# Sharing the products of the first three slots between VectorE and ScalarE, and issuing the fourth load behind the third group

## The chip, the core and the metric

The kernel runs on one core of a Trainium2 chip. Four of its engines matter here. VectorE (DVE in the profile) and ScalarE (ACT) compute; SyncE (SP) computes nothing and issues transfers; ScalarE issues transfers too, from the same instruction stream as its arithmetic. The transfers themselves run on the core's 16 DMA engines. They are fed by two queues: q1 holds what SyncE issued, q10 what ScalarE issued. An engine runs its instructions in order; an instruction that waits holds up all that stand behind it on that engine.

The metric is the time of the kernel on the device in microseconds (us), the median of several runs. The profile shows one further execution, whose own time stands beside its span below.

## The reference

For each of 16 x 1024 tokens there is a row of 512 fp32 numbers and two fp32 weights. The result has, for each token, two rows of 512: the token's row times its first weight and times its second. `expert_indices` is not used.

```python
batch, seq, hidden, n_experts = 16, 1024, 512, 8
k = 2
x_expanded = x[:, :, np.newaxis, :].repeat(k, axis=2)
weights = expert_weights[..., np.newaxis]
return (x_expanded * weights).astype(np.float32)
```

33.55 MB are read and 67.11 MB are written, and each element read is multiplied twice.

## The kernel before

The 16384 tokens are cut into 8 groups of 2048. In a group each of the 128 partitions holds 16 consecutive tokens (T = 16). There are three slots in SBUF, and group i uses slot i mod 3. A slot has 64 KB in each partition, which is 16384 fp32 numbers: room for the 16 x 2 product rows of a group. The load of a group (4 MB) brings the 16 x-rows of each partition into the upper half of the slot, numbers 8192 to 16383. The products are then written in place over the whole slot: token t reads 512 numbers from 8192 + 512 t and writes 1024 numbers from 1024 t. So the products of tokens 0 to 7 go into the free lower half, and those of the tokens behind them overwrite x-rows that must have been used: token 11 writes over the rows of tokens 6 and 7, token 12 over those of 8 and 9, token 13 over 10 and 11, token 14 over 12 and 13, and token 15 over 14 and its own.

`products` (line 133) is one VectorE instruction, a `tensor_tensor` multiply for a run of tokens lo to hi, with the weights broadcast along the row. `ranges` (line 123) cuts the 16 tokens into runs of 8, 4, 2 and 1, so that no run overwrites a row that it still reads; with the 16th token left, `last` (line 151) does its two products on ScalarE, two instructions of 128 x 512, the second of them in place. They come after all four VectorE instructions of the group.

Stores go out on SyncE: one of 8 MB for a whole group (line 178), but for the first group and the last group two of 4 MB, of which the first (line 174) follows the run of 8 tokens. Loads go out on ScalarE (line 120). The first three loads are issued at the start. Load i + 2 stands in ScalarE's stream behind the two products of group i, for i from 1, and it waits there until the stores of group i - 1, which used the same slot, have landed. So ScalarE's stream is: loads 0, 1, 2; two products of group 0; two of group 1; load 3; two of group 2; load 4; two of group 3; load 5; and so on. The order of all instructions is that of the program, since the kernel schedules by hand (line 104).

Ahead of the groups, the weights (128 KB) are loaded on SyncE and turned into their layout `w_tile` by TensorE transposes and three VectorE copies (lines 66 to 102).

Of the kernel before, what the change touches and what calls it, by code (L numbers as in the profile page):

```python
# [1 line left out]

# [4 lines left out]


@with_exitstack
def kernel(  # L10
    ctx: ExitStack,
    tc: tile.TileContext,
    x: bass.AP,
    expert_indices: bass.AP,
    expert_weights: bass.AP,
    out: bass.AP,
):
    nc = tc.nc

    batch, seq, hidden = x.shape  # L20
    k = expert_weights.shape[-1]
    P = nc.NUM_PARTITIONS
    ntok = batch * seq
    assert ntok % P == 0

    f32 = mybir.dt.float32
    row = k * hidden


    groups = [16] * 8  # L30
    assert sum(groups) * P == ntok
    TX = max(groups)

    xf = x.rearrange("b s h -> (b s) h")
    of = out.rearrange("b s k h -> (b s) (k h)")
    wf = expert_weights.rearrange("b s k -> (b s) k")

    w_pool = ctx.enter_context(tc.tile_pool(name="w_pool", bufs=1))
    slots = ctx.enter_context(tc.tile_pool(name="slots", bufs=3))
    raw_pool = ctx.enter_context(tc.tile_pool(name="raw_pool", bufs=1))  # L40
    psum = ctx.enter_context(
        tc.tile_pool(name="psum", bufs=2, space=bass.MemoryType.PSUM)
    )

    w_tile = w_pool.tile([P, sum(groups) * k], f32)

    def rows(flat, done, T):
        return flat[done * P : (done + T) * P, :].rearrange("(p a) n -> p (a n)", a=T)

    B = 8
    M = P // B
    ident = w_pool.tile([P, P], f32)
    nc.gpsimd.memset(ident, 0.0)  # L55
    nc.gpsimd.affine_select(  # L56
        out=ident,
        in_=ident,
        compare_op=mybir.AluOpType.not_equal,
        fill=1.0,  # L60
        base=0,
        pattern=[[-1, P]],
        channel_multiplier=1,
    )

    def weights_in(head, G, T):
        raw_tile = raw_pool.tile([G * M, B * T * k], f32, name=f"raw{T}_tile")
        nc.sync.dma_start(
            out=raw_tile,
            in_=wf[head * P : (head + G * T) * P, :].rearrange(  # L70
                "(q a) n -> q (a n)", a=B * T
            ),
        )
        return raw_tile

    def weights_spread(raw_tile, head, G, T):
        n = T * k
        col_tile = raw_pool.tile([n, G * P], f32, name=f"col{T}_tile")
        cols = col_tile.rearrange("c (q r) -> c q r", r=B)
        step = 4  # L80
        for r0 in range(0, B, step):
            up_tile = psum.tile([n, step, G * M], f32)
            for r in range(step):
                nc.tensor.transpose(  # L84
                    up_tile[:, r, :],
                    raw_tile[:, (r0 + r) * n : (r0 + r + 1) * n],
                    ident[: G * M, : G * M],
                )
            nc.vector.tensor_copy(  # L89
                out=cols[:, :, r0 : r0 + step],  # L90
                in_=up_tile.rearrange("c r q -> c q r"),
            )
        down_tile = psum.tile([P, G * n], f32)
        for g in range(G):
            nc.tensor.transpose(  # L95
                down_tile[:, g * n : (g + 1) * n],
                col_tile[:, g * P : (g + 1) * P],
                ident[:n, :n],
            )
        nc.vector.tensor_copy(  # L100
            out=w_tile[:, head * k : (head + G * T) * k], in_=down_tile
        )

    ctx.enter_context(tc.manual_schedule())

    starts = [sum(groups[:i]) for i in range(len(groups))]
    loaded = []

    def load(i):
        if i >= len(groups):
            return
        T = groups[i]
        slot_tile = slots.tile([P, TX * row], f32)
        loaded.append(slot_tile)
        src = rows(xf, starts[i], T)
        at = T * (row - hidden)
        nc.scalar.dma_start(out=slot_tile[:, at : at + T * hidden], in_=src)  # L120


    def ranges(T):
        lo, out = 0, []
        while lo < T - 1:
            hi = lo + 1
            while (hi + 1) * k <= T * (k - 1) + lo and hi < T - 1:
                hi += 1
            out.append((lo, hi))
            lo = hi  # L130
        return out

    def products(slot_tile, T, lo, hi, w_at):
        m = hi - lo
        at = T * (row - hidden) + lo * hidden
        nc.vector.tensor_tensor(  # L136
            out=slot_tile[:, lo * row : hi * row].rearrange(
                "p (t k h) -> p t k h", t=m, k=k
            ),
            in0=slot_tile[:, at : at + m * hidden]  # L140
            .rearrange("p (t h) -> p t h", t=m)
            .unsqueeze(2)
            .to_broadcast([P, m, k, hidden]),
            in1=w_tile[:, w_at + lo * k : w_at + hi * k]
            .rearrange("p (t k) -> p t k", t=m)
            .unsqueeze(3)
            .to_broadcast([P, m, k, hidden]),
            op=mybir.AluOpType.mult,
        )

    def last(slot_tile, T, w_at):
        for c in range(T * k - k, T * k):
            nc.scalar.mul(  # L153
                out=slot_tile[:, c * hidden : (c + 1) * hidden],
                in_=slot_tile[:, T * row - hidden : T * row],
                mul=w_tile[:, w_at + c : w_at + c + 1],
            )

    raw_tile = weights_in(0, 8, 16)
    load(0)  # L160
    load(1)
    load(2)
    weights_spread(raw_tile, 0, 8, 16)

    for i, T in enumerate(groups):
        slot_tile = loaded[i]
        outr = rows(of, starts[i], T)
        w_at = starts[i] * k
        done = 0
        for lo, hi in ranges(T):  # L170
            products(slot_tile, T, lo, hi, w_at)
            if i in (0, len(groups) - 1) and done == 0:
                done = hi
                nc.sync.dma_start(
                    out=outr[:, : done * row], in_=slot_tile[:, : done * row]
                )
        last(slot_tile, T, w_at)
        nc.sync.dma_start(
            out=outr[:, done * row :], in_=slot_tile[:, done * row : T * row]
        )  # L180
        if i:
            load(i + 2)

# [1 line left out]
_INS = ['x', 'expert_indices', 'expert_weights']  # L185
_OUTS = [((16, 1024, 2, 512), 'float32')]


# [23 lines left out]
```

## Time and profile before

| what | value |
|---|---|
| median of three runs | 242.16 us (239.26 to 251.51; 239.26, 242.16, 251.51) |
| the profiled execution's own time | 239.3 us |
| its span in the profile | 237.5 us |
| VectorE busy | 134.7 us (57%) |
| ScalarE busy | 12.8 us (5%) |
| TensorE busy | 2.9 us |
| moved by DMA | 100.80 MB, 424 GB/s over the span |
| the 16 DMA engines' time, q1 and q10 | 65.5% and 33.2% |

Times in the rows of the profile count from the start of the span. In a row of the timeline the first number is the start, the second the length, "x4" means four instructions merged, and the bracket tells how long the engine had been idle and what ended that. An issue ("ACTq", "SPq") is the short instruction that hands a transfer to its queue; the transfer runs on by itself and "lands" when its semaphore has been raised by all 16 engines. In a table of windows the columns are: the stretch, its length, the busy time of PE, PEld, DVE, ACT and POOL with the number of instructions, the granted TensorE clock, the busy share of the 16 DMA engines and the rate in GB/s. The share can pass 1.00 a little, since a packet's bytes and time are booked at one place.

### The profile page before, as it was taken

Reading aid. Unit: us, or ns where it says so; the run is one execution under the profiler, and the core shown is the slowest. Engines: PE = TensorE matmul, PEld = TensorE weight load, DVE = VectorE, ACT = ScalarE, POOL = GpSimd, SP = SyncE. Lnnn points to the kernel's source line nnn. Section 1 sums busy time; section 2 is a strip of 40 time slices with the busy share of each in tenths; the row PEclk is TensorE's granted clock in tenths of the full one; section 3 lists DMA queues with packets and bytes.
Section 4 is the critical chain, followed back from the end, with each engine's and each line's share of the span. In section 5 each row is a group of like instructions: output and inputs, shape, how many; then the busy total and the mean of one; then the engine's idle time right before and its main releaser. Section 6 shows DMA issues by size and latency. Waiting matters only on the chain.

```text
span 237.5 us, 184 instructions
## 1 busy us (share of the span) xinstructions
PE 2.9 (1%) x16; PEld 1.9 (1%) x16; DVE 134.7 (57%) x35; ACT 12.8 (5%) x17; POOL 0.7 (0%) x6
## 2 busy tenths in 40 slices
PE   0400000000000000000000000000000000000000
PEld 0300000000000000000000000000000000000000
DVE  0289999999600089900998009970199602995000
ACT  0020020110200000020001100020000200002000
POOL 1000000000000000000000000000000000000000
DMA  7999999999899899899799898998998989989996
GB/s 284 444 441 441 353 441 441 436 447 441 375 419 530 353 441 530 353 441 530 337 458 430 370 524 353 441 530 353 441 530 348 447 386 453 486 353 441 441 441 265
DMA packets 2736, 100.80 MB, mean 424 GB/s; under 512 B 304, under 2 KB 432, under 8 KB 432
## 3 DMA queue, kind: packets, MB, share of 16 engines
q1 hardware_dynamic: 1584, 67.24, 65.5%
q10 hardware_dynamic: 1152, 33.55, 33.2%
HBM read 33.69 MB, written 67.11 MB: 424 GB/s over the span
## 4 chain that ended last, share of the span: by engine, by line
DMA 61%; DVE 28%; ACT 2%; issue 0%; DVEq 0%; ACTq 0%
DMA slot_tile<-in_x_dram 33%; DMA out_dram<-slot_tile 29%; DVE slot_tile L136 28%; ACT slot_tile L153 2%; DVEq L136 0%; ACTq L120 0%
## 5 line engine op out<-in xcount | busy, mean ns | idle before, releaser
L136 DVE TENSOR_TENSOR slot_tile<-slot_tile,w_tile 128x8192 f32<-128x8192 f32 (+3 forms) x32 | 132.9, 4158 | 71.6 <-DMA slot_tile<-in_x_dram 70.7
L153 ACT ACTIVATE slot_tile<-slot_tile,w_tile 128x512 f32<-128x512 f32 x16 | 11.5, 721 | 192.5 <-DVE slot_tile L136 192.3
L89 DVE COPY col_tile<-up_tile 32x512 f32<-32x512 f32 x2 | 1.4, 678 | 9.6 <-PE up_tile L84 9.6
L153 ACT ACT_TABLE_LOAD x1 | 1.3, 1283 | 13.2 <-DMA slot_tile<-in_x_dram 13.2
L84 PE MATMUL up_tile<-ident,raw_tile 128*32 128x128 f32 x8 | 1.9, 411 | 8.4 <-DMA raw_tile<-in_expert_weights_dram 8.4
L84 PEld LDWEIGHTS up_tile<-ident,raw_tile 128*32 128x32 f32 x8 | 1.0, 135 | 8.8 <-issue 8.4
L100 DVE COPY w_tile<-down_tile 128x256 f32<-128x256 f32 x1 | 0.4, 424 | 1.1 <-PE down_tile L95 1.1
L95 PE MATMUL down_tile<-ident,col_tile 32*128 32x32 f32 x8 | 1.1, 292 | 0.8 <-DVE col_tile L89 0.8
L95 PEld LDWEIGHTS down_tile<-ident,col_tile 32*128 32x128 f32 x8 | 0.9, 214 | 1.3 <-DVE col_tile L89 1.3
L56 POOL TENSOR_SCALAR_AFFINE_SELECT ident<-ident 128x128 f32<-128x128 f32 x1 | 0.3, 292 | 0.1
L55 POOL MEMSET ident<- 128x128 f32 x1 | 0.2, 204 | 0.3 <-POOLq L196 0.3
L196 POOL MEMSET const-bfloat16-1.0<- 128x1 bf16 x1 | 0.1, 101 | 0.0
L196 POOL MEMSET const-uint8-127<- 128x1 uint8 x1 | 0.1, 101 | 0.0
L196 POOL MEMSET const-float32-0.0<- 128x1 f32 x1 | 0.1, 98 | 0.2 <-issue 0.2
L196 POOL MEMSET const-float32-1.0<- 128x1 f32 x1 | 0.1, 98 | 0.0
## 6 DMA issues: line engine op xcount, KB each, us to landing
slot_tile<-in_x_dram ACTq DMA_DIRECT2D x8, 4096.0 KB, 32.6
out_dram<-slot_tile SPq DMA_DIRECT2D x4, 4096.0 KB, 19.5
raw_tile<-in_expert_weights_dram SPq DMA_DIRECT2D x1, 128.0 KB, 7.5
out_dram<-slot_tile SPq DMA_DIRECT2D x6, 35.9
```

The costliest lines, as they stand in the source:

```text
L55: nc.gpsimd.memset(ident, 0.0)
L56: nc.gpsimd.affine_select(out=ident, in_=ident, compare_op=mybir.AluOpType.not_equal, fill=1.0, base=0, pattern=[[-1, P]], channel_multipl ...
L84: nc.tensor.transpose(up_tile[:, r, :], raw_tile[:, (r0 + r) * n : (r0 + r + 1) * n], ident[: G * M, : G * M],)
L89: nc.vector.tensor_copy(out=cols[:, :, r0 : r0 + step], in_=up_tile.rearrange("c r q -> c q r"),)
L95: nc.tensor.transpose(down_tile[:, g * n : (g + 1) * n], col_tile[:, g * P : (g + 1) * P], ident[:n, :n],)
L100: nc.vector.tensor_copy(out=w_tile[:, head * k : (head + G * T) * k], in_=down_tile)
L136: nc.vector.tensor_tensor(out=slot_tile[:, lo * row : hi * row].rearrange("p (t k h) -> p t k h", t=m, k=k), in0=slot_tile[:, at : at + m ...
L153: nc.scalar.mul(out=slot_tile[:, c * hidden : (c + 1) * hidden], in_=slot_tile[:, T * row - hidden : T * row], mul=w_tile[:, w_at + c : w_ ...
L196: nc = _bacc.Bacc("TRN2", target_bir_lowering=False, num_devices=1)
```

## The change

In the groups 0, 1 and 2 (`shared`) the products are divided anew. Group 0: VectorE does tokens 0 to 7 in one instruction and 8 to 10 in another; ScalarE does token 11 and token 12; VectorE does 13 and 14 in one instruction each, and token 15 in two `tensor_scalar` instructions of 128 x 512. Groups 1 and 2: VectorE does tokens 0 to 4; ScalarE does tokens 5, 6 and 7; VectorE does 8 to 11; ScalarE does 12; VectorE does 13, 14 and, with `tensor_scalar`, 15. Each token on ScalarE is two instructions of 128 x 512, of the form that `last` had. Groups 3 to 7 (`vector_alone`) are divided as before.

The places of the stores are as before. Load 3 no longer stands behind the products of group 1: it stands behind those of group 2, with load 4 right behind it. ScalarE's stream is then: loads 0, 1, 2; four products of group 0; eight of group 1; eight of group 2; load 3; load 4; two of group 3; load 5; and so on.

What follows from the layout of the slot: token 12 on ScalarE waits until VectorE has read rows 8 and 9; token 14 on VectorE waits until ScalarE has read row 12; in groups 1 and 2 VectorE's tokens 8 to 11 overwrite the rows 0 to 7 and wait until ScalarE has read rows 5, 6 and 7. In group 0 token 13 waits until ScalarE has read row 11.

```diff
-    def last(slot_tile, T, w_at):
-        for c in range(T * k - k, T * k):
-            nc.scalar.mul(
...
+    def scaled(eng, slot_tile, T, t, w_at):
+        at = T * (row - hidden) + t * hidden
+        for c in range(t * k, t * k + k):
+            out = slot_tile[:, c * hidden : (c + 1) * hidden]
+            x_in = slot_tile[:, at : at + hidden]
+            w = w_tile[:, w_at + c : w_at + c + 1]
+            if eng is nc.scalar:
+                eng.mul(out=out, in_=x_in, mul=w)
+            else:
+                eng.tensor_scalar(
+                    out=out, in0=x_in, scalar1=w, scalar2=None, op0=mybir.AluOpType.mult
+                )
+
+    def vector_alone(i, slot_tile, T, w_at):
+        products(slot_tile, T, 0, 8, w_at)
+        yield
+        products(slot_tile, T, 8, 12, w_at)
+        products(slot_tile, T, 12, 14, w_at)
+        products(slot_tile, T, 14, 15, w_at)
+        scaled(nc.scalar, slot_tile, T, 15, w_at)
+
+    def shared(i, slot_tile, T, w_at):
+        if i == 0:
+            products(slot_tile, T, 0, 8, w_at)
+            yield
+            products(slot_tile, T, 8, 11, w_at)
+            scaled(nc.scalar, slot_tile, T, 11, w_at)
+        else:
+            products(slot_tile, T, 0, 5, w_at)
+            for t in range(5, 8):
+                scaled(nc.scalar, slot_tile, T, t, w_at)
+            yield
+            products(slot_tile, T, 8, 12, w_at)
+        scaled(nc.scalar, slot_tile, T, 12, w_at)
+        products(slot_tile, T, 13, 14, w_at)
+        products(slot_tile, T, 14, 15, w_at)
+        scaled(nc.vector, slot_tile, T, 15, w_at)
...
-        for lo, hi in ranges(T):
-            products(slot_tile, T, lo, hi, w_at)
-            if i in (0, len(groups) - 1) and done == 0:
-                done = hi
+        for _ in (shared if i < 3 else vector_alone)(i, slot_tile, T, w_at):
+            if i in (0, len(groups) - 1):
+                done = T // 2
...
-        last(slot_tile, T, w_at)
         nc.sync.dma_start(
             out=outr[:, done * row :], in_=slot_tile[:, done * row : T * row]
         )
-        if i:
+        if i == 2:
+            load(3)
+        if i >= 2:
             load(i + 2)
```

More of the change, by code (lines that the diff above doesn't have):

```diff
@@ L120, in load @@
         nc.scalar.dma_start(out=slot_tile[:, at : at + T * hidden], in_=src)
[L123 to L131, printed above, removed]
     def products(slot_tile, T, lo, hi, w_at):
@@ L149, in products @@
         )
-    def last(slot_tile, T, w_at):
-        for c in range(T * k - k, T * k):
[L153 to L157, printed above, removed]
+    def scaled(eng, slot_tile, T, t, w_at):
[33 more added lines that the diff above has]
+        scaled(nc.vector, slot_tile, T, 15, w_at)
     raw_tile = weights_in(0, 8, 16)
```

## The prediction

> **What bounds the kernel now.** I read the head of the page first, then its DMA queues, then the busy shares stretch by stretch, then the two issuing engines' timelines.
>
> ```profile
> span 237.5 us, 184 instructions
> ...
> PE 2.9 (1%) x16; PEld 1.9 (1%) x16; DVE 134.7 (57%) x35; ACT 12.8 (5%) x17; POOL 0.7 (0%) x6
> ...
> DMA packets 2736, 100.80 MB, mean 424 GB/s; under 512 B 304, under 2 KB 432, under 8 KB 432
> ...
> q1 hardware_dynamic: 1584, 67.24, 65.5%
> q10 hardware_dynamic: 1152, 33.55, 33.2%
> ```
>
> The two queues together take 98.7% of the time that 16 DMA engines have in the span. No arithmetic engine is near that: DVE is at 57%. That is an average, so I look where the missing 1.3% lies.
>
> ```profile
> 0.00:2.50 2.50, 0.00 (x0) 0.00 (x0) 0.00 (x0) 0.00 (x0) 0.70 (x6) 1.00 0.56 147
> 2.50:48.00 45.50, 2.92 (x16) 1.93 (x16) 36.37 (x12) 4.07 (x5) 0.00 (x0) 1.00 1.00 421
> 48.00:57.00 9.00, 0.00 (x0) 0.00 (x0) 8.97 (x2) 0.10 (x1) 0.00 (x0) 1.00 1.00 433
> 57.00:100.00 43.00, 0.00 (x0) 0.00 (x0) 21.78 (x7) 1.44 (x2) 0.00 (x0) 1.00 1.00 434
> 100.00:200.00 100.00, 0.00 (x0) 0.00 (x0) 50.93 (x13) 5.77 (x8) 0.00 (x0) 1.00 1.02 440
> 200.00:236.00 36.00, 0.00 (x0) 0.00 (x0) 16.64 (x4) 1.44 (x2) 0.00 (x0) 1.00 0.94 408
> 236.00:237.50 1.50, 0.00 (x0) 0.00 (x0) 0.00 (x0) 0.00 (x0) 0.00 (x0) 1.00 0.00 0
> ```
>
> The last two columns carry the argument. From 2.5 us to 236 us the 16 engines are busy without a gap (1.02 and 0.94 are the two sides of one boundary); only the first 2.5 us and the last 1.5 us are not full. The bytes are fixed by the reference, and so is the rate while the queues are full: 434 GB/s between 57 and 100 us, with DVE busy half of the time. The kernel is at the floor of its transfers, and a change of the arithmetic can only win back a gap in the transfers, of which this execution has none, or open one.
>
> **The change, step by step.** First the prices and the present order.
>
> ```profile
> L136 DVE TENSOR_TENSOR slot_tile<-slot_tile,w_tile 128x8192 f32<-128x8192 f32 x8 | 69.5, 8691 | 70.7 <-DMA slot_tile<-in_x_dram 70.7
> L136 DVE TENSOR_TENSOR slot_tile<-slot_tile,w_tile 128x4096 f32<-128x4096 f32 x8 | 35.4, 4425 | 0.3
> L136 DVE TENSOR_TENSOR slot_tile<-slot_tile,w_tile 128x2048 f32<-128x2048 f32 x8 | 18.3, 2292 | 0.3
> L153 ACT ACTIVATE slot_tile<-slot_tile,w_tile 128x512 f32<-128x512 f32 x16 | 11.5, 721 | 192.5 <-DVE slot_tile L136 192.3
> L136 DVE TENSOR_TENSOR slot_tile<-slot_tile,w_tile 128x1024 f32<-128x1024 f32 x8 | 9.8, 1225 | 0.3
> ...
> L89 DVE COPY col_tile<-up_tile 32x512 f32<-32x512 f32 x2 | 1.4, 678 | 9.6 <-PE up_tile L84 9.6
> ```
>
> ```profile
> 0.74 1.37 ACTq L120 DMA_DIRECT2D slot_tile<-in_x_dram  x3
> ...
> 29.98 1.48 ACT L153 ACTIVATE slot_tile<-slot_tile,w_tile 128x512 f32<-128x512 f32 x2 [15.52 <-DVE slot_tile L136]
> 46.63 1.48 ACT L153 ACTIVATE slot_tile<-slot_tile,w_tile 128x512 f32<-128x512 f32 x2 [15.17 <-DVE slot_tile L136]
> 52.81 0.33 ACTq L120 DMA_DIRECT2D slot_tile<-in_x_dram  x1
> 63.27 1.48 ACT L153 ACTIVATE slot_tile<-slot_tile,w_tile 128x512 f32<-128x512 f32 x2 [15.17 <-DVE slot_tile L136]
> 80.57 0.33 ACTq L120 DMA_DIRECT2D slot_tile<-in_x_dram  x1
> 101.05 1.48 ACT L153 ACTIVATE slot_tile<-slot_tile,w_tile 128x512 f32<-128x512 f32 x2 [36.31 <-DVE slot_tile L136]
> 109.53 0.33 ACTq L120 DMA_DIRECT2D slot_tile<-in_x_dram  x1
> ```
>
> ```profile
> 13.21 50.03 DVE L136 TENSOR_TENSOR slot_tile<-slot_tile,w_tile 128x8192 f32<-128x8192 f32 x12 [0.66 <-DMA slot_tile<-in_x_dram]
> 84.28 16.74 DVE L136 TENSOR_TENSOR slot_tile<-slot_tile,w_tile 128x8192 f32<-128x8192 f32 x4 [21.05 <-DMA slot_tile<-in_x_dram]
> ```
>
> Two VectorE rows give a line: (8691 - 4425) / 4096 = 1.04 ns an element and 0.16 us fixed; 1024 elements come to 1.23 us, as the row has it. So 3072 elements take an estimated 3.36 us and 5120 take 5.49 us. A ScalarE token is the pair of 1.48 us. `tensor_scalar` of 128x512 is not in this trace. Its bound above is the 128x1024 product, 1.23 us each, below it is zero; I take 0.69 us each by the line (the 512-element copy at 0.678 us lies beside it), 1.40 us for the pair of token 15.
>
> [...]
>
> Group 0: VectorE 13.21 to 21.91 (tokens 0 to 7, the first store unmoved), 8 to 10 until 25.3; ScalarE token 11 beside it, token 12 from 25.3 to 26.8; VectorE 13 until 26.5, 14 from 26.8 to 28.0, 15 until 29.5. The second store goes at 29.5; now it goes when ScalarE's pair ends, 29.98 + 1.48 = 31.5.
>
> Group 1: VectorE 0 to 4 until 35.0. ScalarE's six products (4.4 us) can start at 26.8; at 29.98 VectorE starts group 1 today without a wait, so load 1 is in by then, and they end by 34.4. Tokens 8 to 11 until 39.4, ScalarE's 12 until 40.9, VectorE's 14 until 42.2, 15 until 43.6. Store 1 goes at 43.6 instead of 48.1.
>
> ```profile
> DMA to landing us min/median/max: 12.4/32.6/39.0
> ```
>
> Group 2: this row is that of the loads. 39.0 us belongs to the last of the three that are issued at 0.74 to 2.11 us (load 3 takes 84.28 - 52.81 = 31.5), so load 2 is in by 41.1. ScalarE's six run from 41.1 to 45.5; VectorE 0 to 4 from 43.6 to 49.1, 8 to 11 until 53.6, ScalarE's 12 until 55.1, VectorE's 15 until 57.7. Store 2 goes at 57.7 instead of 63.27 + 1.48 = 64.8.
>
> **Load 3** is the step that moves the wrong way. Today it goes at 52.81, when the store of group 0 has landed. Afterwards it stands behind ScalarE's token 12 and goes at 55.1, D = 2.3 us later. With `tensor_scalar` at zero it would be held by the landing again, D = 0; at 1.23 us (two pairs lie ahead of it) D = 4.4. Behind it on ScalarE are load 4, which waits for store 1 (80.57 today), group 3's pair and load 5.
>
> What is D worth? Store 1 is in q1 from 43.6, store 2 from 57.7, so the engines have 16.8 MB to move, 39 us at 434 GB/s, whether load 3 comes at 52.8 or 55.1. What load 3 loses in those 2.3 us, the store gains. The next place is group 3: it starts when load 3 has landed (84.28) and its store goes at 101.05 + 1.48 = 102.5, so at 104.8 with D. By that time the transfers ahead are five loads and three stores, 5 x 4.19 + 3 x 8.39 = 46.1 MB: 0.4 MB by 2.5 us, 19.2 by 48, 3.9 by 57, and the rest at 434 GB/s until about 109.1. From the issue of the first loads to full flow pass 0.74 to 2.5 us, 1.8 us, so store 3 must be issued by about 107.3. It has 4.8 us of margin today and 2.5 afterwards. Load 5 comes at the landing of store 2 (109.53 today) in both. No gap; the step costs nothing, and each microsecond of D above 4.8 costs one.
>
> Groups 3 to 7 keep their instructions, and their cycle is one of 12.6 MB, 29 us (80.57 to 109.53), against 18.3 us from landing to store (84.28 to 102.5). The end is unmoved: in the windows from 100 to 236 us the engines never run dry.
>
> **Sum.** Earlier stores 0, 1, 2: nothing, since the engines are full when they come; they only queue earlier. Load 3: nothing. Together 0.0 on the profiled execution's span of 237.5 us and its 239.3 us, with 1 us either way for the stretch until 48 us, where the rate is 421 instead of 434 (3% of 45.5 us is 1.4 us). That execution equals the fastest of the three runs shown; their median is 242.16, and the profile has no row for the rest. I take the middle of 239.3 and 242.16, 240.7 us.
>
> **Rivals.** *Faster: store 1 has been coming late in other executions.* Today it is issued 52.81 - 48.13 = 4.7 us ahead of the landing of the store before it, the thinnest lead in the first half, and a VectorE start only a few microseconds later would leave the engines dry around 50 us. The chain of waits passes there:
>
> ```profile
> 46.63 0.73 ACT slot_tile L153
> ...
> 48.13 32.36 DMA out_dram<-slot_tile
> ```
>
> The change makes the lead 9.2 us. Against it: the window 48 to 57 is full, 1.00. If the 2.9 us between 239.3 and the median are such gaps, the changed kernel comes to 239.3, 1.2% below the median; over 2% only where the kernel before measures above 244.2. *Slower: load 3 late enough to dry both queues.* The place is ScalarE's stream at group 2, the price one for one above D = 4.8. It decides if VectorE's first product and ScalarE's six do not run side by side in groups 1 and 2: 2 x 4.4 us more, D = 11.2, a gap of 6.4 us at about 109 us, 245.7 us; with `tensor_scalar` at its upper bound as well D = 13.3 and 247.8. For it: these pairs of instructions have never run for long side by side in the trace. Against it: in the row at 29.98 and that at 46.63 ScalarE runs beside VectorE's next group and takes the 1.48 us that it takes at 101.05 with VectorE idle. *The move does nothing at all:* with `tensor_scalar` at the low end load 3 stays at 52.8, and the time is that of the forecast.
>
> **How the numbers follow.** Two per cent, 4.8 us, is about what a measurement of this kernel can tell from no change, as its three runs lie 12 us apart. Transfers full throughout: 0.70, at 240.7, with 238.5 to 244 of its own (the floor less about 1 us, and the spread). The faster rival 0.10, at 239.3. The slower one 0.20, 245.7 to 247.8. The range runs from 238.5 to 248: below lies only a higher rate of the engines, above a longer gap or a run like the one at 251.51. Of the rivals' cases I count the faster one as faster and the slower one as slower.
>
> **What would show it.** In the changed profile: the DMA share 1.00 from 2.5 to 236 us; store 1 issued near 43.6, load 3 near 55, store 3 before 107.3; DVE busy down to about 127 us (groups 1 and 2 at 13.8 instead of 16.6 us, group 0 at 15.9), ACT up to about 23 us (30 products of 0.721 and the table load); the DVE wait for load 3 grown by some 8 us. A share under 1 near 109 us would prove the slower rival; store 1's earlier issue with a shorter span would prove the faster. A different rate inside full windows would make the prediction wrong in a way that none of these rows foretells.

## The result, and the profile after

| | before | changed |
|---|---|---|
| median on record | 240.77 us (239.26 to 251.51, 6 executions) | 248.19 us (246.68 to 250.53, 6 executions) |
| ratio | | 1.034, 95% interval 1.027 to 1.042: slower |
| profiled execution, span | 237.5 us (its own time 239.3 us) | 245.1 us (its own time 247.13 us) |

The ratio of 1.034 leaves out the executions that lie more than 1.5% above the fastest of their kernel, two of the kernel before (247.24 and 251.51 us) and one of the changed (250.53 us); what sets such executions apart turned out to be the subject of this case.

The head of the page of the changed kernel and its DMA queues:

```profile
span 245.1 us, 207 instructions
...
PE 2.9 (1%) x16; PEld 2.0 (1%) x16; DVE 126.9 (52%) x41; ACT 21.3 (9%) x31; POOL 0.7 (0%) x6
...
DMA packets 2736, 100.80 MB, mean 411 GB/s; under 512 B 304, under 2 KB 432, under 8 KB 432
...
q1 hardware_dynamic: 1584, 67.24, 63.6%
q10 hardware_dynamic: 1152, 33.55, 32.3%
```

Packets and bytes are those of before. VectorE has 7.8 us less to do, as meant. But the queues now fill 95.9% of the engines' time instead of 98.7%, and the span is 7.6 us longer. Where it went shows in ScalarE's issues. First the changed kernel, from the token 12 of group 2 on, then the kernel before (the rows of it that the prediction did not show):

```profile
52.69 0.72 ACT L147 ACTIVATE slot_tile<-slot_tile,w_tile 128x512 f32<-128x512 f32 x1 [8.27 <-DVE slot_tile L124]
52.83 0.33 ACTq L119 DMA_DIRECT2D slot_tile<-in_x_dram  x1
53.32 0.70 ACT L147 ACTIVATE slot_tile<-slot_tile,w_tile 128x512 f32<-128x512 f32 x1
80.57 0.34 ACTq L119 DMA_DIRECT2D slot_tile<-in_x_dram  x1
101.20 1.48 ACT L147 ACTIVATE slot_tile<-slot_tile,w_tile 128x512 f32<-128x512 f32 x2 [47.18 <-DVE slot_tile L124]
109.70 0.34 ACTq L119 DMA_DIRECT2D slot_tile<-in_x_dram  x1
...
141.31 0.33 ACTq L119 DMA_DIRECT2D slot_tile<-in_x_dram  x1
...
172.48 0.33 ACTq L119 DMA_DIRECT2D slot_tile<-in_x_dram  x1
```

```profile
138.49 0.33 ACTq L120 DMA_DIRECT2D slot_tile<-in_x_dram  x1
...
167.53 0.34 ACTq L120 DMA_DIRECT2D slot_tile<-in_x_dram  x1
```

Load 3 goes at 52.83 (52.81 before), load 4 at 80.57 (80.57), load 5 at 109.70 (109.53). So at 110 us, when every changed instruction has long been done, nothing is lost. Load 6 is then 2.8 us late and load 7 5.0 us. The loss arises in groups 4 to 7, whose instructions are the same in both kernels. What lacks there is not work in the queues. Windows of the changed kernel, columns as before:

```profile
141.00:172.00 31.00, 0.00 (x0) 0.00 (x0) 16.64 (x4) 1.44 (x2) 0.00 (x0) 1.00 1.02 438
...
216.00:217.40 1.40, 0.00 (x0) 0.00 (x0) 1.36 (x2) 0.00 (x0) 0.00 (x0) 1.00 0.49 211
...
236.90:243.50 6.60, 0.00 (x0) 0.00 (x0) 0.00 (x0) 0.00 (x0) 0.00 (x0) 1.00 0.06 25
```

In the last 6.6 us before the last transfer lands the share is 0.06. One engine of sixteen is 1/16 = 0.0625. The transfer view of the same stretch has its packets:

```profile
q1 hardware_dynamic: 12, 0.16, 5.8%
```

Fifteen engines are done at 236.9 us, hardly later than in the kernel before (share 0.00 from 236.0 us on), and one works alone until 243.5 us. The store issued at 132.18 us has 15 of its 16 signals by 166.30 us and the last at 172.46, and load 7, which waits for its landing, goes at 172.48: the landing came as late as the last engine. At 216 us the others run dry for want of the next store (share 0.49), issued at 216.53, which had to wait for the products of load 7 (landed at 207.69). Until 203 us the share of the windows, a mean over 16 engines, stays at 1.00 to 1.02, although one engine is 7.0 us behind at 190 us (below): its longer packets count as busy (a 64 KB packet at 121.1 us takes 3.20 us instead of 2.42), and it hides in the mean.

To see when it falls behind I put the packets of the trace into 16 chains, each packet behind the one that ended as it began, and took for each moment how much work the hindmost chain has done less than the median one (in us of an engine's work, at the usual 1.21 us for a packet of 32 KB and 2.42 us for one of 64 KB, the medians in the traces of both kernels; where two chains cross the assignment is not certain). The second trace is that of a_again, below.

```
us into the span            55    80   108   125   135   190
before                     0.2   0.2   0.2   0.2   0.2   0.2
changed                    0.2   0.2   0.4   2.0   2.6   7.0
changed (second trace)     1.1   1.9   2.4   3.3   4.7   8.8
```

In the first trace some 15 packets of that engine take longer from 80 us on, by 0.2 to 0.8 us each on top of the usual 1.21 us (32 KB) or 2.42 us (64 KB), while those of the other engines keep theirs. I call this a lag. It need not be one engine alone: in the trace of a_third, below, the share from 239.5 to 243.0 us is 0.17, close to three engines of sixteen (0.19), and the last of the 40 slices of its page moves 48 GB/s against 16 in the first trace.

### The profile page after: what moved, and what is told of

Same layout as the page of the kernel before. It is cut to its first block, busy times and chain, and to the rows that moved or that the text cites. A ratio compares the mean times of both kernels' runs of the same rounds, so it can differ in the third digit from the quotient of the medians.

```text
span 245.1 us, 207 instructions
## 1 busy us (share of the span) xinstructions
PE 2.9 (1%) x16; PEld 2.0 (1%) x16; DVE 126.9 (52%) x41; ACT 21.3 (9%) x31; POOL 0.7 (0%) x6
## 4 chain that ended last, share of the span: by engine, by line
DMA 65%; DVE 25%; ACT 2%; issue 0%; DVEq 0%; ACTq 0%; SPq 0%
DMA slot_tile<-in_x_dram 33%; DMA out_dram<-slot_tile 32%; DVE slot_tile L124 24%; ACT slot_tile L147 2%; DVE slot_tile L149 1%; DVEq L124 0%; ACTq L119 0%; SPq L197 0%
## 5 line engine op out<-in xcount | busy, mean ns | idle before, releaser
L124 DVE TENSOR_TENSOR slot_tile<-slot_tile,w_tile 128x1024 f32<-128x1024 f32 (+5 forms) x32 | 122.4, 3825 | 86.5 <-DMA slot_tile<-in_x_dram 85.2
L147 ACT ACTIVATE slot_tile<-slot_tile,w_tile 128x512 f32<-128x512 f32 x30 | 20.0, 714 | 191.5 <-DVE slot_tile L124 191.1
L149 DVE TENSOR_SCALAR slot_tile<-slot_tile,w_tile 128x512 f32<-128x512 f32 x6 | 2.9, 486 | 0.2
```

The lines of the kernel that those rows point to most:

```text
L124: nc.vector.tensor_tensor(out=slot_tile[:, lo * row : hi * row].rearrange("p (t k h) -> p t k h", t=m, k=k), in0=slot_tile[:, at : at + m ...
L147: eng.mul(out=out, in_=x_in, mul=w)
L149: eng.tensor_scalar(out=out, in0=x_in, scalar1=w, scalar2=None, op0=mybir.AluOpType.mult)
```

## The experiments

Each measured time below stands beside the kernel before, run on the same chip in turn with it; those executions, 68 with the ones above, make a sample of their own: 239.26 to 251.66 us, median 246.9, with 11 below 240 us (median 239.4), 15 between 240 and 246, and 42 above (median 247.5). The sample above had been lucky: in its 6, 4 lay below 246. I count executions below 246 us as those with little lag. For executions without a trace that is read from the time alone.

### Which part makes it late: four variants

Stores 0, 1 and 2 put back to about their old times (e1_hold; 34.1, 49.9 and 67.4 us in its trace, 31.5, 48.1 and 64.8 in the kernel before): each waits on SyncE for a small transfer behind idle ScalarE products.

```diff
...
+    def gate(n):
+        for _ in range(n):
+            nc.scalar.mul(out=junk_tile, in_=zero_tile, mul=w_tile[:, 0:1])
+        nc.sync.dma_start(out=junk_tile[:1, :256], in_=wf[:128, :].rearrange("(q a) n -> q (a n)", a=128))
...
+            if held:
+                gate(2 if i == 1 else 5)
+                store(*held.pop())
...
```

> The changed kernel with its arithmetic and its load order, but the stores of groups 0, 1 and 2 are held on SyncE by a 1 KB gate transfer that waits for idle ScalarE products (2, 5 and 15 of about 0.7 us), so that they go at about 31, 48 and 65 us as in the kernel before. Queue theory (the stores queued early, 42.8 and 56.4 us, let one of the 16 DMA engines fall behind): 239 to 240 us and no lagging engine. Arithmetic theory (the new instructions on ScalarE and VectorE, or their code, do it): 247 to 250 us. Chance theory (any kernel of this kind falls into the lag in some executions): some runs at 239 and some at 247 to 251.

Measured: 247.57 to 251.21 us, 4 executions. Not the 239.4 of the queue theory; but the three small transfers in q1 may themselves be a disturbance, so this says little.

Idle ScalarE products in the kernel before (e2_pad):

```diff
...
+        if i < 3:
+            idle_work((2, 6, 6)[i])
         last(slot_tile, T, w_at)
```

> The kernel before with 14 more ScalarE products (2, 6 and 6 in groups 0, 1 and 2) of a scratch tile in time that ScalarE spends idle; no store, load or slot instruction moves. Queue theory: as before, 239 to 242 us. Arithmetic theory: 247 to 250 us. Chance theory: the same scatter as the kernel before.

Measured: 247.90 to 249.74 us, 4 executions, the hindmost engine 3.8 us behind at 135 us. By itself that spoke for the arithmetic theory. But the kernel before, beside it: 247.37, 247.74, 247.22, 246.43, 248.28, 239.43 and 251.60 us. The unchanged kernel lags too, mostly.

Early stores without sharing (e3_early; products of groups 0 to 2 left out):

```diff
-        for lo, hi in ranges(T):
+        for lo, hi in ranges(T)[: (3, 2, 2)[i] if i < 3 else None]:
```

> The kernel before with VectorE's last products left out in groups 0 (token 14), 1 and 2 (tokens 12 to 14 each), so that their stores go out at about 30, 43.5 and 57 us; no ScalarE sharing, no tensor_scalar, load 3 behind group 1. Those products are not computed. Queue theory: 247 to 250 us with one engine lagging. Arithmetic theory: 239 to 240 us. Chance theory: scatter.

Measured: 239.50, 245.25, 246.80, 248.32 us. A mixture, as the chance theory had it: early stores (28.9, 41.9 and 55.0 us in the trace of the 239.50) do not cost time in themselves.

Load 3 back behind group 1 (e4_order):

```diff
-        if i == 2:
-            load(3)
-        if i >= 2:
+        if i:
             load(i + 2)
```

> The changed kernel with load 3 back behind group 1 as in the kernel before: ScalarE stands at load 3 until 52.8 us, so group 2's tokens 5 to 7 come late and store 2 goes at about 66 us, store 1 still at 43. If store 2 queued early is what matters: 239 to 240 us; if store 1 or the arithmetic: 247 to 250 us. If the order of the load itself were the cause: 239 to 240 us too, and e3_early tells the two apart.

Measured: 239.60, 239.61, 239.84 and 247.01 us: with shared products and store 1 at 42.7 us, 239.6 is reached. Neither the sharing nor the early store 1 costs anything when nothing lags.

### What a lag needs: packets and queues

The changed kernel once more (a_again), unaltered:

> The changed kernel once more, unaltered. Lag theory (every kernel of this family runs either at about 239.4 us or, where one of the 16 DMA engines lags, at 246 to 251 us, and the change sets neither the two times nor which one comes): executions at 239 to 240 among those at 246 to 251, as the kernel before shows beside it. Theory that the change brings the lag about: none at 239 to 240, while the kernel before has some.

Measured: 247.12 to 249.12 us (4), beside the kernel before with one of 7 at 239.47 and the rest at 246.06 to 249.75.

The variant e4_order once more (e4_again), unaltered:

> The changed kernel with load 3 behind group 1, once more, unaltered: three of its four executions were at 239.6 to 239.8 us. Theory that the order of load 3 or the time of store 2 decides on the lag: again most at 239.6. Lag theory by chance: the same mixture as the other kernels, so that executions at 246 to 251 us are as frequent as in the kernel before.

Measured: 240.16, 244.79, 249.05, 249.79 us.

Stores cut into halves (e5_halves), in the kernel before:

```diff
-        nc.sync.dma_start(
-            out=outr[:, done * row :], in_=slot_tile[:, done * row : T * row]
-        )
+        for lo in range(done, T, T // 2):
+            hi = lo + T // 2
+            nc.sync.dma_start(
+                out=outr[:, lo * row : hi * row], in_=slot_tile[:, lo * row : hi * row]
+            )
```

> The kernel before with each 8 MB store cut into two of 4 MB issued one behind the other, so that its packets are 32 KB like those of the loads, and a busy engine alternates between equals. If the lag comes from 64 KB store packets taking turns with 32 KB load packets: 239 to 240 us in all executions, no engine behind the others. If packet size is not it: the same mixture of 239.4 and 246 to 251 us. Load 3 would land sooner, since it gets half instead of a third of the engines.

Measured: 240.07 to 241.18 us in all 4 executions. All packets of the loads and stores are of 32 KB now.

One queue (e6_oneq), in the kernel before:

```diff
-        nc.scalar.dma_start(out=slot_tile[:, at : at + T * hidden], in_=src)
+        nc.sync.dma_start(out=slot_tile[:, at : at + T * hidden], in_=src)
```

> The kernel before with the loads issued on SyncE, so that loads and stores stand in one queue and an engine does not take turns between two. If the lag needs two queues taking turns: 239 to 240 us in all executions. If it does not: the same mixture of 239.4 and 246 to 251 us. SyncE waits at load 3 until 52.8 us and store 2 is behind it, which by the trace of before costs nothing, as store 2 goes at 64.8.

Measured: 241.81 to 243.52 us in all 4. Its queue row, all bytes in q1:

```profile
q1 hardware_dynamic: 2736, 100.80, 98.0%
```

In the trace of the changed kernel the engines take turns between the queues: from 57 to 77 us each of the 16 chains has 64 KB packets of q1 and 32 KB packets of q10 in turn. Both ways out of taking turns between 64 KB and 32 KB packets end the large lag (241.18 and 243.52 us at worst), and beside them the kernel before had 6 of 7 above 246 us. No run here explains why an engine should slow down in taking turns. Nor is the size of the packets quite separated from what goes with it: with halved stores the loads land sooner (a median of 22.9 us from issue to landing in e5_again, below, instead of 32.6), and no run has packets of 64 KB in both queues.

### The change where nothing lags, and a lag on purpose

The changed kernel with the halved stores of e5_halves (e7_after_halves), and e5_halves again:

> The changed kernel with every 8 MB store cut into two of 4 MB, as in e5_halves, where no execution lagged. Theory that the change itself is worth nothing and the 248 us come from the lag: the time of e5_halves beside it, 240 to 241 us, within 0.5%. Theory that the change costs time by itself: 246 us or more here too.

> The kernel before with halved stores, unaltered, as the partner of e7_after_halves: 240 to 241.2 us in all executions, while the kernel before goes on mixing 239.4 and 246 to 251 us.

Measured, 12 executions each: 241.10 us median (240.08 to 241.68) with the change, 240.00 us (239.46 to 240.92) without. Against the executions of the kernel before at 242 us or less the ratios are 1.0021 (0.9984 to 1.0058) and 1.0018 (0.9995 to 1.004). The change wins nothing here, as forecast. Side by side it is even a little slower, by 0.9 us in the mean (95% interval 0.5 to 1.4 us), and no run shows why. The kernel before beside them: 26 executions, 239.38 to 249.27 us, median 244.6. The windows of e7_after_halves:

```profile
57.00:100.00 43.00, 0.00 (x0) 0.00 (x0) 17.73 (x7) 1.44 (x2) 0.00 (x0) 1.00 1.00 432
100.00:200.00 100.00, 0.00 (x0) 0.00 (x0) 54.98 (x13) 4.33 (x6) 0.00 (x0) 1.00 1.00 433
200.00:236.00 36.00, 0.00 (x0) 0.00 (x0) 11.56 (x4) 1.44 (x2) 0.00 (x0) 1.00 0.99 429
236.00:239.30 3.30, 0.00 (x0) 0.00 (x0) 0.00 (x0) 0.00 (x0) 0.00 (x0) 1.00 0.05 20
```

An engine is late here too, but not by 7 us: 0.05 in the last row is an estimated 2.6 us of one engine's work (0.05 x 16 x 3.3 us).

A delay planted in the kernel before (e8_seed), and in e5_halves (e9_seed_halves):

```diff
     load(2)
+    nc.sync.dma_start(
+        out=loaded[2][:2, : 16 * hidden], in_=xf[:32, :].rearrange("(p a) n -> p (a n)", a=16)
+    )
```

> The kernel before with one transfer more at the start: 32 KB of x into each of two partitions of the still unused lower half of slot 2, so that one or two of the 16 DMA engines have 1.2 us more to do than the others from the first microseconds on; all else as before. Theory that an engine which is out of step by over about half a microsecond loses more and more where 32 KB and 64 KB packets take turns: no execution at 239 to 241, all at 246 us or more. Theory that being out of step does no harm: 239.4 + 1.2 = 240.6 us in the executions that do not lag, about as many as in the kernel before.

> The same extra transfer in the kernel with halved stores. Theory that the growth needs packets of two sizes: 241 to 243 us (240.9 and the 1.2 us), no execution above 244. If equal packets let the lag grow as well: 246 us or more.

Measured: e8_seed 247.21 to 249.24 us, all 4; e9_seed_halves 241.15 to 242.37 us, all 6. For e8_seed a window in which only the late engines still work, for e9_seed_halves the last one:

```profile
239.20:244.40 5.20, 0.00 (x0) 0.00 (x0) 0.00 (x0) 0.00 (x0) 0.00 (x0) 1.00 0.12 50
```

```profile
236.50:239.60 3.10, 0.00 (x0) 0.00 (x0) 0.00 (x0) 0.00 (x0) 0.00 (x0) 1.00 0.05 21
```

```
us into the span            20    55    80   108   125   135   190
before, delay planted      2.0   1.7   1.9   2.5   3.7   5.0   7.8
halved, delay planted      2.0   1.7   1.8   1.8   1.6   1.6   1.5
```

The planted packets are not counted as work in this table; there are two, of 32 KB, they took 1.74 and 1.83 us, and they ran on two engines. The planted 2.0 us grow to 7.8 where two sizes take turns, and do not grow where all packets are equal. Four of four above 246 us could still be chance, about once in 15, since 12 of the 26 of the kernel before beside them lay above 246 us. But the trace has two late engines at the end (share 0.12, 2/16 = 0.125), and at 190 us the two hindmost chains are the two that got the planted packets, both 7.8 us behind, the next one 1.7; picked by chance, two of sixteen would be these two once in 120. So the two engines that were put out of step by 2.0 us fell further behind, to 7.8 us: that is a cause of the loss and not only its sign. The growth is not steady: until 80 us there is none, and then it goes on for 110 us. Nor does it need a planted delay: in the first trace of the changed kernel the hindmost engine was 0.2 us behind until 80 us.

### Does the change make the lag likelier?

Three kernels once more, unaltered: the changed one (a_third), e2_pad (e2_again) and e4_order (e4_third).

> The changed kernel, unaltered, for the share of executions that lag: so far 10 of 10 are at 246.7 us or more. Theory that lag comes by chance as in the kernel before: about a quarter of the executions at 239 to 241 us and half below 246.6, as in the kernel before with its 26. Theory that the change makes the lag likelier: at most one or two of twelve below 246.6 us.

> The kernel before with 14 idle ScalarE products, unaltered: 4 of 4 were at 247.9 us or more. If more ScalarE work in the first 60 us makes the lag likelier: most of twelve at 246 us or more. If those four were chance: the mixture of the kernel before.

> The changed kernel with load 3 behind group 1, unaltered: 4 of 8 were at 239.6 to 240.2 us. If it lags as seldom as this again, while the changed kernel always lags, the lag hangs on load 3 and store 2, not on the shared products; if it shows the mixture of the kernel before, nothing can be read from its first runs.

Only group 0 shared (e10_group0), load 3 behind group 1 as in e4_order:

```diff
-        for _ in (shared if i < 3 else vector_alone)(i, slot_tile, T, w_at):
+        for _ in (shared if i < 1 else vector_alone)(i, slot_tile, T, w_at):
...
```

> The changed kernel with only group 0 shared and load 3 behind group 1: store 0's second half goes at 29 instead of 31.5 us, the rest like before. If the sharing in group 0, beside the first store, where the traces show an engine fall out of step, is what makes the lag likelier: most of twelve at 246 us or more. If not: the mixture of the kernel before.

Measured, 6 executions each: a_third 246.44 to 251.40 us, median 247.6; e2_again 242.35 to 248.44, median 247.1; e4_third 239.53 to 248.07, median 246.6; e10_group0 239.50 to 249.31, median 245.5; the kernel before beside them, 11 executions, 242.05 to 249.84, median 247.1.

Store 2 alone put back (e11_hold2; load 3 stays behind token 12), and store 2 alone made early in the kernel before, tokens 8 to 14 of its group not computed (e12_early2):

```diff
+        if i == 2:
+            load(3)
...
-        scaled(nc.vector, slot_tile, T, 15, w_at)
+        if i < 2:
+            scaled(nc.vector, slot_tile, T, 15, w_at)
+        else:
+            for _ in range(14):
+                nc.scalar.mul(out=junk_tile, in_=zero_tile, mul=w_tile[:, 0:1])
+            scaled(nc.scalar, slot_tile, T, 15, w_at)
...
```

```diff
-        for lo, hi in ranges(T):
+        for lo, hi in ranges(T)[: 1 if i == 2 else None]:
```

> The changed kernel with store 2 alone put back to about 65 us: load 3 at its place behind token 12 of group 2, then 14 idle ScalarE products into a scratch tile, then group 2's token 15 on ScalarE instead of VectorE. Theory that store 2, queued at 56.4 us behind a store 1 that has hardly begun, makes the lag likelier: the mixture of the kernel before, several executions below 246 us. Theory that it is the position of load 3 in ScalarE's stream or the shared products: nearly all at 246.4 us or more, as in 16 of 16 of the changed kernel.

> The kernel before with VectorE's tokens 8 to 14 of group 2 left out (not computed), so that store 2 alone goes early, at about 57 us; all else as before. Theory that the early store 2 makes the lag likelier: nearly all executions at 246 us or more. Theory that it does not: the mixture of the kernel before (24 of 57 below 246 us).

Measured, 6 executions each: e11_hold2 242.08 to 251.87 us, median 248.0; e12_early2 245.60 to 248.57, median 247.4; the kernel before beside them 243.53 to 251.66, median 247.5.

All executions with 64 KB stores in two queues and without a planted delay, and the kernel before beside them:

| kernel | below 246 us | range, us | before beside it, below 246 us |
|---|---|---|---|
| changed (record, a_again, a_third) | 0 of 16 | 246.44 to 251.40 | 9 of 24 |
| load 3 behind group 1 (e4_order, _again, _third) | 8 of 14 | 239.53 to 249.79 | 6 of 25 |
| group 0 alone shared (e10_group0) | 3 of 6 | 239.50 to 249.31 | 4 of 11 |
| early stores, no sharing (e3_early) | 2 of 4 | 239.50 to 248.32 | 1 of 7 |
| idle ScalarE products (e2_pad, e2_again) | 2 of 10 | 242.35 to 249.74 | 5 of 18 |
| stores put back behind small transfers (e1_hold) | 0 of 4 | 247.57 to 251.21 | 1 of 7 |
| store 2 alone put back (e11_hold2) | 1 of 6 | 242.08 to 251.87 | 2 of 11 |
| store 2 alone early (e12_early2) | 2 of 6 | 245.60 to 248.57 | 2 of 11 |

The bound of 246 us is rough: the execution of e4_third at 245.75 us counts as below, and its trace has five engines 3 to 4 us late at the end. The changed kernel has lagged each time. If it had the share of the kernel before, 9 of 40 in all, none in 16 would come by chance about once in 200; without the record's own executions, in which the kernel before was lucky, it would be 5 of 28, and none in 10 would come once in 11. So the change may well make the lag likelier, but that is not shown. The variant that puts load 3 back, and with it store 2 to 65 us, lags least of all (8 of 14 below 246). Beyond that nothing is settled. Store 2's early place in the queue was the last suspect: taking it away gave one execution at 242.08 and five at 246.3 or more, giving it to the kernel before gave two at 245.6 and 245.9. Neither stands apart from the kernel before beside it. Load 3's position in ScalarE's stream cannot act through its time, since it goes at 52.8 us in both. The share also differs from session to session with the same kernel (1 of 7, 14 of 26) and with the chip: the sessions up to e9_seed_halves ran on one chip, the two behind them on two others, where none of the 22 executions of the kernel before lay below 242 us. So with 6 executions a variant can't be told from another. What starts the lag, and what in the change raises its share, stays open.

## Why the prediction was wrong

**The floor was right, and so was the cost of each edit.** Rows of the changed kernel's table by shape:

```profile
L124 DVE TENSOR_TENSOR slot_tile<-slot_tile,w_tile 128x4096 f32<-128x4096 f32 x7 | 31.0, 4425 | 0.4
L147 ACT ACTIVATE slot_tile<-slot_tile,w_tile 128x512 f32<-128x512 f32 x30 | 20.0, 714 | 191.5 <-DVE slot_tile L124 191.1 <-DMA slot_tile<-in_x_dram 0.2
...
L124 DVE TENSOR_TENSOR slot_tile<-slot_tile,w_tile 128x5120 f32<-128x5120 f32 x2 | 11.0, 5485 | 0.0
L124 DVE TENSOR_TENSOR slot_tile<-slot_tile,w_tile 128x3072 f32<-128x3072 f32 x1 | 3.4, 3357 | 0.0
L149 DVE TENSOR_SCALAR slot_tile<-slot_tile,w_tile 128x512 f32<-128x512 f32 x6 | 2.9, 486 | 0.2
```

The line through two rows gave 5.49 and 3.36 us for the new sizes; they are 5.485 and 3.357. `tensor_scalar`, taken at 0.69 us between bounds of 0 and 1.23, takes 0.486. Store 1 was put at 43.6 us and store 2 at 57.7. The chain of waits and SyncE's timeline of the changed kernel:

```profile
42.79 37.69 DMA out_dram<-slot_tile
```

```profile
56.39 0.33 SPq L197 DMA_DIRECT2D out_dram<-slot_tile  x1
```

Store 1 goes at 42.8 and store 2 at 56.4. DVE was to be busy about 127 us (126.9), ACT about 23 (21.3). ScalarE's and VectorE's timelines:

```profile
25.45 5.01 ACT L147 ACTIVATE slot_tile<-slot_tile,w_tile 128x512 f32<-128x512 f32 x8 [2.06 <-DVE slot_tile L124]
```

```profile
42.64 12.64 DVE L124 TENSOR_TENSOR slot_tile<-slot_tile,w_tile 128x5120 f32<-128x5120 f32 x4
```

Eight products in a row took ScalarE 5.01 us, not the 5.9 of four pairs.

**Load 3: D is 0, not 2.3.** Two pairs of `tensor_scalar` at 1.01 us instead of 1.40 and the closer products of ScalarE bring token 12 to 52.69. Nor does load 3, which stands behind token 12's two products, wait for their end (53.32 + 0.70 = 54.02), as the prediction had it: it goes at 52.83, 0.1 us behind the landing of store 0, as before. That is the low end of the bounds. So ScalarE's starts did not keep to the order of its stream there; what stands behind a waiting load did wait, in e4_order, where load 3 goes at 52.77 us and group 2's six products behind it start at 53.15, against 40.63 in the changed kernel. The slower rival, ScalarE and VectorE not side by side, did not happen: VectorE's four products of group 2 took 12.64 us in the row above, and 5.49 + 4.43 + 2 x 1.23 = 12.4 us is what they take alone. Store 3 goes at 101.20 + 1.48 = 102.7, well ahead of 107.3. The rival named "the move does nothing at all" held.

**The step that failed is the floor's own sentence: "The bytes are fixed by the reference, and so is the rate while the queues are full".** The rate holds for the engines in step (1.21 and 2.42 us a packet). The time ends with the last of sixteen engines, and that one's packets got slower while both queues were full: 7.0 us of work behind at 190 us, 6.6 us late at the end. The mean share of 1.00 could not show it. The prediction closed with a rate that changes inside full windows as what no row foretells; there was no price and no chance for it, although the three times of the kernel before, 239.26, 242.16 and 251.51, lay 12 us apart and the profile was of the fastest. That spread was a second way in which this kernel runs, half of its executions or more, and I used it only to put the forecast 1.4 us higher and the ends of the range further out, not as a rival with a price and a chance.

**The rival of a late store 1**, by which the kernel before would lose time around 50 us, had its sign right in that the kernel before often runs longer, and its mechanism wrong: e3_early and the changed kernel have store 1 at 41.9 and 42.8 us and lag all the same, e3_early in some executions.

**So how much is the change worth?** Without a lag nothing, or a loss of up to about 1 us, by e7_after_halves beside e5_again; the nearest variant with 64 KB stores, e4_order, reaches 239.6. Where both lag, also next to nothing: 247.7 us is the median of the changed kernel's 16, 247.5 that of the 42 executions of the kernel before above 246. The 3.4% on record are the distance between the two ways of running, and the changed kernel's share in it is how often it takes the worse one.

## What to carry to other kernels

Here a mean share of 1.00 to 1.02 over 16 engines until 203 us was not a floor: one engine was 7.0 us behind at 190 us, and the last 6.6 us before the last landing, with a share of 0.06, were its own. In a kernel at the limit of its transfers, look at the last microseconds of the span and at the spread of the plain times (239.26 to 251.51 us here), before you trust the fastest profile. In this kernel the sizes of the packets decided more than any order of the arithmetic: cutting the 8 MB stores in two, so that loads and stores both move in 32 KB packets, gave 240.0 us as a median of 12 and 240.9 at worst (241.2 in the 4 executions of the other session), where the kernel before had a median of 244.6 and 249.3 at worst beside the 12. A handful of executions can't tell a change from a kernel that runs in two ways; in the first six, the kernel before showed 240.8, and in 68 it showed 246.9.

## What the runs showed of the hardware

- One of the 16 DMA engines fell from 0.4 us behind the median at 108 us to 7.0 at 190 in the changed kernel (in a_again, the second trace, from 2.4 to 8.8), in full queues, where 32 KB packets of one queue and 64 KB packets of another took turns. With 32 KB packets only, the share at the end was 0.01 from 236.0 to 237.7 us (e5_again) and 0.05 from 236.0 to 239.3 us (e7_after_halves), with one queue 0.06 from 236.0 to 240.0 us (e6_oneq): an estimated 0.3, 2.6 and 3.8 us of one engine's work.
- A delay of 2.0 us planted on two engines grew to 7.8 us on both at 190 us in the first case (e8_seed); with 32 KB packets only it did not grow (2.0 us at 20 us, 1.5 at 190, e9_seed_halves).
- ScalarE and VectorE, each on its own tokens of the same slot, did not slow each other in the changed kernel: VectorE's two 128x5120 products, of which 1.4 and 1.8 us ran beside ScalarE's, took 5485 ns where the line through the products of the kernel before gives 5.49 us, and ScalarE's products took 714 ns in the mean, against 721 before.
- A load that stands behind two products in ScalarE's stream was issued before they had ended: at 52.83 us in the changed kernel, with the second product from 53.32 to 54.02 (in e7_after_halves at 54.62, with the second from 55.16). Six products that stand behind a load which waits until 52.77 us started at 53.15 (e4_order).
- fp32 `tensor_scalar` of 128x512 with a weight for each partition took 486 ns in the changed kernel.
